# Gate and up products by seven block products in place of eight, in a two-layer hybrid decoder trunk

## The chip, the cores and the metric

The kernel runs on one core of a Trainium2 chip. The metric is the device time of one execution in microseconds (us). The engines go by the profile's names: PE is TensorE (PEld its weight loads), DVE is VectorE, ACT is ScalarE, POOL is GpSimd, SP is the engine that issues the transfers.

## What is computed

Two layers, each of a mixer (latent attention beside a state space part) and a feed-forward part, over 512 rows of 1024 columns in float32. The change concerns the feed-forward part:

```
h = rmsnorm(x, norm2_w[l]) * (1.0 + sc2) + sh2
x = x + g2 * swiglu(h, w_gate_up[l], w_down[l])

def swiglu(h, w_gate_up, w_down):
    g, u = jnp.split(h @ w_gate_up, 2, axis=-1)
    return (jax.nn.silu(g) * u) @ w_down
```

The inner width is 2816, which is 22 tiles of 128. The six modulation vectors of a layer (sh2, sc2, g2 among them) come from a product of the condition c with a 1024 x 6144 matrix.

## The kernel before, in words

Activations lie transposed: the 1024 columns on 8 tiles of partitions, the 512 rows along the free dimension (xT, hh, hl). Every float32 product is made of three matmuls of a reduced format: each operand is split into hi (a cast, on ACT) and lo (source minus hi, on DVE or POOL), and `mm3` (L317) adds hi·hi, hi·lo and lo·hi in PSUM. A weight tile of 128 columns is 512 KB; `wload` (L304) has SP load it into one of three raw buffers, ACT cast it to hi and DVE or POOL subtract to lo; a table of bits says which of the two.

The second norm's sums of squares and the hidden are made half by half (`HALVES`, 256 rows each). `out_proj` gives the second half of the mixer's output; beside it the first half's hidden is made. Then `nst`, a matmul with ones, gives the second half's mean square, ACT and DVE turn it into a row scale, and `hid` (L420) makes the hidden per k: one step on DVE (ht), one cast with a bias on ACT (hh), one step on DVE (hl).

`ffn` (L1013) then runs over f, the 22 tiles of the inner width. Per f there is a gate tile and an up tile, each 8 blocks of k, three matmuls of 512 columns per block: 48 matmuls. ACT takes silu of the gate's PSUM (sg), DVE multiplies by the up's PSUM, and `split` (L440) makes ah and al, of which all 22 tiles are kept. The first two tiles are run in halves (`mtiles_halves`, L449), so that the first half's matmuls can run while the second half's hidden is made. From f = 2 on, layer 0 also loads the next layer's modulation matrix, three tiles per f, 48 in all; each costs DVE a multiply with a sum (`ada1`, rawa). At last the down products run: 8 tiles m of 22 blocks of k, 66 matmuls of 512 columns each (dps), the last m in halves, and DVE adds each to xT.

The order on each engine is the scheduler's, which places instructions by their data; only the mixer's part is pinned. PSUM has five banks of the kind mm and three of the kind ms here.

## Time and profile before

| | |
|---|---|
| time, median of 3 executions | 1289.55 us (1289.34 to 1289.65) |
| span of the profiled execution | 1284.9 us |
| mean granted PE clock, core 0 | 0.974 |
| PE busy | 1211.4 us (94%) |
| DVE, ACT, POOL busy | 634.1, 519.9, 531.1 us |
| gate and up products, layer 0 | from 306.25 to 550.29 us |
| gate and up products, layer 1 | from about 916 to 1158.29 us |
| down products, layer 1 | from 1158.29 to the end |

The span is the time from the first to the last instruction of one profiled execution. The times of a row are starts from the beginning of the span, with a duration; a matmul's duration is longer than its distance from the next one, because matmuls are pipelined, so costs of PE are read as distances from start to start. "granted clock" is 1.00 where PE runs at 2.4 GHz and falls towards 0.5 where it runs at 1.2 GHz.

### The profile page before, as it was taken

To read this page: it belongs to the slowest core of one execution; us is meant where nothing else is said; L and a number is where in the kernel's file an instruction comes from. 1 tells how busy PE (TensorE), PEld (TensorE's weight loads), DVE (VectorE), ACT (ScalarE), POOL (GpSimd) and SP (SyncE) were. 2 spreads that over 40 slices of the span, in tenths; PEclk is the share of its full clock that TensorE was granted. 3 is DMA by queue.
4 is the path that set the end of the run, shared out by engine and by line. 5 is a ranking of instruction groups with operands and counts; after the bars stand their busy time and mean duration, and the time that the engine had idled before them with its cause. 6 is when DMAs were issued, how large, how long until landed. Compare 5 with 4: busy or idle time off the path is not lost. (4 is left out here: it accounts for less than half of the span.)

```text
span 1284.9 us, 16463 instructions
## 1 busy us (share of the span) xinstructions
PE 1211.4 (94%) x6343; PEld 1005.1 (78%) x6344; DVE 634.1 (49%) x1128; ACT 519.9 (40%) x896; POOL 531.1 (41%) x310
## 2 busy tenths in 40 slices
PE   6889796889999999999998999979999999999998
PEld 6768674689888888888887887659988888888888
DVE  6979778879245545211128885576821111110100
ACT  4366774435322222222226668654532222222110
POOL 2651145263676666523333232346333333333231
PEclk9899898899999999999999899999999999999999
DMA  9433352464477777423223222103333332323331
GB/s 321 154 125 102 114 164 99 150 200 143 129 241 238 239 240 237 134 87 97 96 71 107 83 79 70 34 33 91 124 115 99 90 106 84 102 94 107 115 101 40
DMA packets 47855, 162.34 MB, mean 126 GB/s; under 512 B 5344, under 2 KB 8224, under 8 KB 47776
## 3 DMA queue, kind: packets, MB, share of 16 engines
q1 hardware_dynamic: 47776, 161.29, 38.8%
q8 instruction: 50, 0.82, 0.3%
q14 instruction: 29, 0.24, 0.1%
HBM read 159.14 MB, written 2.13 MB: 126 GB/s over the span
## 5 line engine op out<-in xcount | busy, mean ns | idle before, releaser
L292 POOL TENSOR_TENSOR lo<-raw,hi 128x1024 fp32r<-128x1024 f32 x108 | 272.6, 2524 | 338.6 <-ACT hi L156 338.5
L156 ACT CAST hi<-raw 128x1024 fp32r<-128x1024 f32 x179 | 188.0, 1051 | 500.8 <-issue 183.5
L140 PE MATMUL gup<-hl,hi 128*128 128x512 f32 (+1 forms) x736 | 280.4, 381 | 0.0
L140 PE MATMUL gup<-hh,lo 128*128 128x512 f32 (+1 forms) x736 | 279.9, 381 | 0.0
L140 PE MATMUL gup<-hh,hi 128*128 128x512 f32 (+1 forms) x736 | 278.6, 381 | 0.0
L156 DVE TENSOR_TENSOR lo<-raw,hi 128x1024 fp32r<-128x1024 f32 x71 | 88.9, 1253 | 152.6 <-ACT hi L156 150.8
L140 PEld LDWEIGHTS gup<-hh,lo 128*128 128x128 f32 x736 | 139.1, 189 | 26.5
L140 PEld LDWEIGHTS gup<-hl,hi 128*128 128x128 f32 x736 | 139.0, 189 | 26.0 <-DVE hl L156 0.2
L140 PEld LDWEIGHTS gup<-hh,hi 128*128 128x128 f32 x736 | 138.4, 189 | 26.2
L156 DVE SCALAR_TENSOR_TENSOR rawa<-rawa,cb 128x1024 f32<-128x1024 f32 x77 | 111.0, 1443 | 76.7 <-DMA rawa<-wada 76.5
L140 PE MATMUL dps<-ah,hi 128*128 128x512 f32 x308 | 121.8, 396 | 0.0
L140 PE MATMUL dps<-al,hi 128*128 128x512 f32 x308 | 121.8, 396 | 0.0
L140 PE MATMUL dps<-ah,lo 128*128 128x512 f32 x308 | 121.8, 396 | 0.0
L156 DVE TENSOR_TENSOR sg<-sg,gup 128x512 f32<-128x512 f32 x44 | 30.3, 688 | 179.6 <-PE gup L140 173.5
L440 POOL TENSOR_TENSOR al<-sg,ah 128x512 fp32r<-128x512 f32 x44 | 67.6, 1535 | 97.2 <-ACT ah L156 93.6
L140 PE MATMUL ops<-hh,hi 128*128 128x256 f32 x256 | 74.4, 290 | 3.1 <-ACT hi L156 1.5
L140 PE MATMUL ops<-hl,hi 128*128 128x256 f32 x256 | 72.5, 283 | 1.0 <-POOL hl L440 1.0
L140 PE MATMUL wps<-hh,hi 128*128 128x512 f32 x168 | 70.8, 422 | 2.4 <-DVE xbc L156 2.4
L140 PE MATMUL ops<-hh,lo 128*128 128x256 f32 x256 | 72.5, 283 | 0.3 <-POOL lo L292 0.3
L140 PEld LDWEIGHTS dps<-al,hi 128*128 128x128 f32 x308 | 57.9, 188 | 14.1
L140 PEld LDWEIGHTS dps<-ah,hi 128*128 128x128 f32 x308 | 57.9, 188 | 14.0
L140 PEld LDWEIGHTS dps<-ah,lo 128*128 128x128 f32 x308 | 57.9, 188 | 13.9
(303 smaller groups left out, 2103.3 us busy)
## 6 DMA issues: line engine op xcount, KB each, us to landing
raw<-ws SPq DMA_DIRECT2D x181, 512.0 KB, 3.5
rawa<-wada SPq DMA_DIRECT2D x80, 512.0 KB, 4.4
raws<-wada SPq DMA_DIRECT2D x16, 512.0 KB, 5.3
ar<-ard SPq DMA_DIRECT2D x8, 512.0 KB, 3.9
rawk<-ws SPq DMA_DIRECT2D x8, 404.0 KB, 5.4
xT<-xin SPq DMA_DIRECT2D x8, 256.0 KB, 5.9
out<-xT SPq DMA_DIRECT2D x7, 256.0 KB, 2.6
rawr<-ws SPq DMA_DIRECT2D x4, 424.0 KB, 3.2
```

What stands on the lines that cost most here:

```text
L140: self._put(self.tc.nc.tensor.matmul(out, lhsT, rhs, **kw), 4 * n if rhs.dtype == F32 else n)
L156: i = f(*args, **kw)
L292: (eng or ve).tensor_tensor(lo[:, :n], raw[:, :n], hi[:, :n].bitcast(F32), op=ALU.subtract)
L440: (eng or ve).tensor_tensor(lo, src, hi.bitcast(F32), op=ALU.subtract)
```

## The change

The gate and up matrices together are a 2 x 2 block matrix: two halves of the inputs' 1024 columns by the gate and the up tile of one f. The hidden is a 2 x 2 block matrix too: two halves of the columns (k 0 to 3, 4 to 7) by two halves of the rows (H0, H1). Strassen's scheme, in Winograd's form, makes the four result blocks from seven products of blocks rather than eight. Per f there are now seven products of 4 blocks of k and three matmuls of 256 columns, 84 matmuls. In their place come sums of blocks: of the hidden once per layer (B12−B11, B22−B11, B22−B12 and one more, `ts`), of the weights per f (`sums_a`, `sums_b`, four sums of 512 columns on DVE), each then split into hi and lo, and of the results per f (`c11`, `c12`, `c22`, `first`, on 256 columns, after copies on ACT). The PSUM tiles are gx (products 1, 6, 7, 4 one after another, read in between), gy (product 2) and gz (products 5, 3); p5 is a copy of gz after product 5. Before product 3 may add into gz, that copy must have been made.

The gate tile's own hi and lo (hiu, lou) come from three different ways: lo on DVE for f = 0, on POOL for f = 1 and 2, and from f = 3 on as a negated copy of the raw tile on ACT and a transfer issued by POOL that reads the same weights from memory and adds them (`accum_op`). The lower half of the up tile is split by ACT and POOL (vh, vl).

The 22 tiles of ah and al are no longer kept: `PIECES` cuts them into 6, 6, 5 and 5, and after each piece its rows of W_down are multiplied, 8 tiles m of 6 or 5 blocks of k, and added to xT. W_down is laid out in 32 tiles of up to 6 blocks in place of 22 of 8. Only the last piece's last three m run in halves. The next layer's modulation tiles are loaded at other places: in each iteration of the first piece, at odd f after that, and in the down products; eight of them are left for layer 1. PE, DVE and ACT are held in the written order from behind nst to the last piece's last three m (`te.pinned = ve.kept = se.kept = True`). PSUM has banks mm 4, my 2, ms 2. The diff's core:

```diff
+PIECES = ((0, 6), (6, 12), (12, 17), (17, 22))
-    def ffn(l, h):
+    def ffn(l, mix, nrm2, kept):
...
-            for f in range(FT):
-                sg = T(f"sg{l}{f}")
-                gps = gu(2 * f)
-                i = se.activation(sg, gps, AF.Silu)
-                if f > 1:
-                    ada_some(1, fp, i)
-                ups = gu(2 * f + 1)
-                i = ve.tensor_tensor(sg, sg, ups, op=ALU.mult)
-                split(ah[:, f, :], al[:, f, :], sg, ge)
-                if f > 1:
-                    ada_some(2, fp, i)
...
+            def weights(b, name, eng, n=8, t=None):
+                if t is None:
+                    t = load(b, name, n)
+                hi, lo = (wp.tile([P, 8, P], F32R, name=f"{x}{name}", tag=x) for x in ("hi", "lo"))
+                se.copy(hi[:, :n], t[:, :n])
+                if eng is None:
+                    se.activation(lo[:, :n], t[:, :n], AF.Identity, scale=-1.0)
+                    ge.dma_start(lo[:, :n], ws[l, b].rearrange("p (k m) -> p k m", m=P)[:, :n], accum_op=ALU.add)
+                else:
+                    eng.tensor_tensor(lo[:, :n], t[:, :n], hi[:, :n].bitcast(F32), op=ALU.subtract)
+                return hi, lo
...
+            def sums_a(f):
+                if f < FT:
+                    g, u = raw[f]
+                    t, hi = pair(f, 5, 6)
+                    ve.tensor_tensor(t[:, 0:K4], u[:, 0:K4], u[:, K4:KT], op=ALU.add)
+                    ve.tensor_tensor(t[:, K4:KT], t[:, 0:K4], g[:, 0:K4], op=ALU.subtract)
+                    se.copy(hi, t)
...
+            def rest(f, i, eng=None):
+                if f < FT:
+                    t, hi, lo = sf[f, i]
+                    (eng or ve).tensor_tensor(lo, t, hi.bitcast(F32), op=ALU.subtract)
...
+            def product(i, f):
...
+                for k in range(K4):
+                    mm3(ps, whi[:, k], wlo[:, k], xhi[:, k], xlo[:, k], k == 0 and i in (1, 2, 5), k == K4 - 1,
+                        skip_group_check=True)
+                if i == 5:
+                    p5[f] = fp.tile([P, HW], F32, name=f"p5{l}_{f}", tag="p5", bufs=2)
+                    se.copy(p5[f], ps)
...
+            te.pinned = ve.kept = se.kept = True
+            for i in (1, 2):
+                product(i, 0)
+            for k in range(K4):
+                nrm2.apply((None, None), rb2, H1, (k,), full=full(k, 1), pool=hpool)
+            c11(0)
+            ve.tensor_tensor(b[11], b[12], b[11], op=ALU.subtract)
+            se.copy(hh[:, 0:K4, H1], b[11])
+            for i in (1, 2):
+                product(i, 1)
+            loads(2)
+            gate_weights(2, ge)
+            for k in range(K4, KT):
+                nrm2.apply(hid_hl, rb2, H1, (k,), full=full(k, 1), pool=hpool)
+                if k == K4:
+                    ve.tensor_tensor(hl[:, 0:K4, H1], b[11], hh[:, 0:K4, H1].bitcast(F32), op=ALU.subtract)
+            c11(1)
+            ve.tensor_tensor(b[11], b[22], b[11], op=ALU.subtract)
+            split(*ts[2], b[11])
+            sums_b(1)
+            for i in (1, 2):
+                product(i, 2)
+            c11(2)
+            rest(1, 3)
+            ve.tensor_tensor(b[12], b[22], b[12], op=ALU.subtract)
+            split(*ts[3], b[12], ge)
+            up_weights(1)
+            for i, f in ((5, 0), (5, 1), (3, 0), (3, 1), (6, 0)):
+                product(i, f)
...
+                    for f in range(max(c0, 3), c1):
+                        if f > c0 + 1:
+                            product(4, f - 2)
+                            first(f - 2, c0, ah, al)
+                        if f > c0:
+                            up_weights(f)
+                        if f < c1 - 1:
+                            loads(f + 2)
+                        product(1, f)
+                        sums_a(f + 1)
+                        product(2, f)
+                        c11(f)
+                        rest(f + 1, 5)
+                        product(5, f)
+                        if f > c0:
+                            product(7, f - 1)
+                            c22(f - 1)
+                        if f < c1 - 2:
+                            gate_weights(f + 2)
+                        else:
+                            fetch(f - c1 + 2)
+                        sums_b(f + 1)
+                        product(6, f)
+                        product(3, f)
+                        c12(f)
+                        rest(f + 1, 3)
+                        silu(f)
+                        if c0 == 0 or f % 2:
+                            ada_some(1)
```

Below, rows of the instruction order of the two kernels; a row is the line, the operation, the tile written and the tiles read, and the size. The first place is ACT at the start of layer 0's feed-forward part. Before, from the last of the first half's hidden (ht_0) over the row scale (na) to the second half's hidden (ht_256):

```order
L156 ACTIVATE hh<-ht_0_2920,mods_92 128x256
L156 ACTIVATE na_256_2926<-nst_256_2924,eps 128x256
L156 ACTIVATE na_256_2926<-na_256_2926 128x256
L156 ACTIVATE hh<-ht_256_2932,mods_92 128x256
L156 ACTIVATE hh<-ht_256_2936,mods_92 128x256
```

And of the kernel after, the last 12 of the 22 rows that stand between the row scale and the copy p5 of f = 0 (p_0); b are the blocks of the hidden, t2h and t3h the hi of two block sums, sh_1_3 that of a weight sum, vh_1 that of an up tile:

```order
L154 ACTIVATE hh<-ht_256_3091,mods_92 128x256
L154 ACTIVATE b_2643<-ht_256_3096,mods_92 128x256
L154 ACTIVATE hh<-ht_256_3096,mods_92 128x256
L154 ACTIVATE b_2643<-ht_256_3101,mods_92 128x256
L154 ACTIVATE hh<-ht_256_3101,mods_92 128x256
L154 COPY sg_3106<-gy_1_3064 128x256
L154 CAST t2h_2631<-b_2640 128x1024
L154 CAST sh_1_3_3113<-sf_1_3_3112 128x1024
L154 COPY sg_3144<-gy_2_3131 128x256
L154 CAST t3h_2633<-b_2641 128x1024
L154 CAST vh_1_3151<-rawxv_1_2987 128x512
L154 COPY p_0_3168<-gz_0_3155 128x256
```

Between the row scale and the first copy out of gz there now stand casts of block sums, of weights and of an up tile, each of them behind the one above it.

The second place is DVE in the middle of layer 1's gate and up products. Before, it has the multiply by the up tile's PSUM and a weight tile's lo now and then:

```order
L156 TENSOR_TENSOR sg_8344<-sg_8344,gup_8383 128x512
L156 TENSOR_TENSOR lo_39_8482<-raw_39_8479,hi_39_8481 128x1024
L156 TENSOR_TENSOR sg_8411<-sg_8411,gup_8450 128x512
L156 TENSOR_TENSOR lo_42_8581<-raw_42_8578,hi_42_8580 128x1024
L156 TENSOR_TENSOR sg_8478<-sg_8478,gup_8517 128x512
```

After, the iteration f = 8 of layer 1 on DVE, from the weight sums of tile 9 to the last step of tile 7:

```order
L154 TENSOR_TENSOR sf_9_5_10733<-rawv_9_10591 128x512
L154 TENSOR_TENSOR sf_9_5_10733<-sf_9_5_10733,rawg_9_10589 128x512
L154 TENSOR_TENSOR sg_10752<-sg_10752,gx_8_10720 128x256
L154 TENSOR_TENSOR sl_9_5_10735<-sf_9_5_10733,sh_9_5_10734 128x1024
L154 TENSOR_TENSOR p_7_10642<-p_7_10642,gx_7_10593 128x256
L154 TENSOR_TENSOR sg_10625<-sg_10625,p_7_10642 128x256
L154 TENSOR_TENSOR sf_9_3_10790<-rawg_9_10589,sf_9_5_10733 128x512
L154 TENSOR_TENSOR sf_9_3_10790<-rawg_9_10589,rawv_9_10591 128x512
L154 TENSOR_TENSOR sg_10752<-sg_10752,gx_8_10720 128x256
L154 TENSOR_TENSOR sl_9_3_10792<-sf_9_3_10790,sh_9_3_10791 128x1024
L154 TENSOR_TENSOR sg_10625<-sg_10625,gx_7_10593 128x256
```

Eleven steps per f stand where one or two stood, and two of them (sl) read what ACT casts (sh) from sums that stand above them. ACT's rows beside it, from silu of tile 7 to silu of tile 8, in the third place:

```order
L154 ACTIVATE sg_10625<-sg_10625 128x512
L154 CAST ah_9688<-sg_10527 128x512
L154 CAST vh_8_10712<-rawxv_8_10493 128x512
L154 CAST sh_9_5_10734<-sf_9_5_10733 128x1024
L154 COPY sg_10752<-gy_8_10739 128x256
L154 COPY p_8_10769<-gz_8_10756 128x256
L154 CAST hiu_10_10785<-rawg_10_10716 128x1024
L154 ACTIVATE lou_10_10786<-rawg_10_10716 128x1024
L154 CAST sh_9_3_10791<-sf_9_3_10790 128x1024
L154 COPY sg_10752<-gz_8_10756 128x256
L154 ACTIVATE sg_10752<-sg_10752 128x512
```

Before, ACT had four rows per f there, in a repeating row of a silu, two casts of weights (hi) and a cast of the activations (ah):

```order
L156 ACTIVATE sg_8344<-gup_8351 128x512
L156 CAST hi_39_8481<-raw_39_8479 128x1024
L156 CAST ah_8026<-sg_8344 128x512
L156 CAST hi_40_8513<-raw_40_8511 128x1024
L156 ACTIVATE sg_8411<-gup_8418 128x512
```

It now has ten, among them two copies out of PSUM (gy, gz) on which DVE's sums into sg wait.

## Rows read from the trace of the kernel before

**Rows 1.** The page, busy time, share of the span and instructions by engine.
```profile
PE 1211.4 (94%) x6343; PEld 1005.1 (78%) x6344; DVE 634.1 (49%) x1128; ACT 519.9 (40%) x896; POOL 531.1 (41%) x310
```

**Rows 2.** Chain that ended last: start, us, engine, tile, line, count; layer 1.
```profile
916.97 2.38 DVE acc L156
...
920.09 238.20 PE gup L140 x1088
1158.29 107.80 PE dps L140 x462
1266.09 7.80 PE dps17mm L140 x66
```

**Rows 3.** Windows: stretch, us, busy PE, PEld, DVE, ACT, POOL, clock, DMA, GB/s.
```profile
310.10:318.00 7.90, 7.84 (x50) 7.75 (x51) 7.26 (x19) 3.94 (x9) 0.00 (x0) 0.78 0.24 66
320.00:550.00 230.00, 230.00 (x1026) 190.88 (x1026) 99.65 (x130) 69.33 (x87) 143.80 (x62) 1.00 0.62 206
...
932.00:1158.20 226.20, 226.20 (x1000) 187.30 (x999) 40.73 (x43) 67.04 (x87) 82.23 (x42) 1.00 0.32 99
```

**Rows 4.** Timeline, PE, layer 0's gate and up: start, us, engine, line, operation, idle before.
```profile
400.01 0.39 PE L140 MATMUL gup<-hh,hi 128*128 128x512 f32 x1
400.24 0.39 PE L140 MATMUL gup<-hl,hi 128*128 128x512 f32 x1
```

**Rows 5.** Timeline, PE, layer 0's output projection, 256 columns, first and eleventh of a row.
```profile
303.01 0.28 PE L140 MATMUL ops<-hh,hi 128*128 128x256 f32 x1
...
304.21 0.28 PE L140 MATMUL ops<-hl,hi 128*128 128x256 f32 x1
```

**Rows 6.** Timeline, start of layer 0's feed-forward part, PE, then DVE, then ACT.
```profile
310.16 0.70 PE L140 MATMUL nst<-acc,ones 128*128 128x256 f32 x2 [1.82 <-DVE acc L156]
...
311.40 0.42 PE L140 MATMUL gup<-hh,hi 128*128 128x256 f32 x1
311.62 0.41 PE L140 MATMUL gup<-hl,hi 128*128 128x256 f32 x1
...
313.29 1.26 DVE L156 SCALAR_TENSOR_TENSOR ht<-xT,gn,nst 128x256 f32<-128x256 f32 x3
...
313.81 1.31 ACT L156 ACTIVATE hh<-ht,mods 128x256 fp32r<-128x256 f32 x3 [1.93 <-DVE ht L156]
```

**Rows 7.** Groups by line and form from 320 us on: count, busy, mean ns, idle before.
```profile
L156 DVE TENSOR_TENSOR lo<-raw,hi 128x1024 fp32r<-128x1024 f32 x50 | 62.8, 1257 | 115.3 <-ACT hi L156 113.5
L156 DVE TENSOR_TENSOR sg<-sg,gup 128x512 f32<-128x512 f32 x43 | 29.6, 688 | 170.8 <-PE gup L140 164.7 <-ACT sg L156 6.1
L156 DVE SCALAR_TENSOR_TENSOR ht<-xT,gn,nst 128x256 f32<-128x256 f32 x32 | 14.1, 474 | 0.2
...
L156 ACT CAST hi<-raw 128x1024 fp32r<-128x1024 f32 x154 | 161.9, 1052 | 486.7 <-issue 183.5 <-PE gup L140 161.6 <-PE dps L140 127.4
L156 ACT CAST ah<-sg 128x512 fp32r<-128x512 f32 x44 | 27.4, 623 | 0.0
...
L156 ACT ACTIVATE hh<-ht,mods 128x256 fp32r<-128x256 f32 x32 | 14.9, 500 | 13.0 <-DVE ht L156 13.0
```

**Rows 8.** Timeline, DVE and POOL in layer 0's gate and up products.
```profile
398.87 1.22 DVE L156 SCALAR_TENSOR_TENSOR rawa<-rawa,cb 128x1024 f32<-128x1024 f32 x1
399.12 3.23 POOL L292 TENSOR_TENSOR lo<-raw,hi 128x1024 fp32r<-128x1024 f32 x1 [3.05 <-ACT hi L156]
...
402.31 1.29 POOL L440 TENSOR_TENSOR al<-sg,ah 128x512 fp32r<-128x512 f32 x1
404.56 2.39 POOL L292 TENSOR_TENSOR lo<-raw,hi 128x1024 fp32r<-128x1024 f32 x1 [0.96 <-ACT hi L156]
404.72 2.25 DVE L156 TENSOR_TENSOR mods<-mods,sm 128x8 f32<-128x8 f32 x1
```

**Rows 9.** The page, queues (packets, MB, share of 16 engines) and issues (KB, us to landing).
```profile
q1 hardware_dynamic: 47776, 161.29, 38.8%
...
raw<-ws SPq DMA_DIRECT2D x181, 512.0 KB, 3.5
```

More of the change, by code (lines that the diff above doesn't have):

```diff
@@ L67 @@
     'OA': (0x82, 0xda),
-    'FW': (0xf, 0x6),
-    'FD': (0xc, 0xe),
     'WU': 18,
@@ L73 @@
     'STK': 2,
-    'FO': (1, 0),
 }
@@ L94 @@
 B_IN, B_UP, B_OUT, B_GU, B_DN = 0, 16, 19, 27, 71
-NBLK = 93
+PIECES = ((0, 6), (6, 12), (12, 17), (17, 22))
+NBLK = 71 + 8 * len(PIECES)
 NR = 424
@@ L334, in ada1 @@
         nc.sync.dma_start(r2, wada[l, t])
-        if te.pinned and t > 15 and PLAN['AD'] & 1 << t - 16:
+        if te.pinned and not ve.kept and t > 15 and PLAN['AD'] & 1 << t - 16:
             n_ = PLAN['AGH']
@@ L415, in hidden, with apply, hid @@
             self.apply(h, self.scale(sl), sl)
-        def apply(self, h, rb, sl, ks=range(KT)):
+        def apply(self, h, rb, sl, ks=range(KT), **kw):
             for k in ks:
-                hid(self.l, self.which, h, k, rb, sl)
-    def hid(l, which, h, k, rb, sl=slice(0, S), eng=None):
+                hid(self.l, self.which, h, k, rb, sl, **kw)
+    def hid(l, which, h, k, rb, sl=slice(0, S), eng=None, full=None, pool=tp):
         o = 0 if which == 1 else 8
@@ L425, in hid @@
         hh, hl = h
-        t = T(f"ht{l}{which}{k}_{sl.start}")
         n = sl.stop - sl.start
+        t = T(f"ht{l}{which}{k}_{sl.start}", [P, n] if pool is not tp else None, pool=pool, **({"bufs": 4} if pool is not tp else {}))
         ve.scalar_tensor_tensor(t[:, :n], xT[:, k, sl], gn[l][:, o + k:o + k + 1], rb[:, :n], op0=ALU.mult, op1=ALU.mult)
+        if full is not None:
+            se.activation(full, t[:, :n], AF.Identity, bias=sh)
+        if hh is None:
+            return
         se.activation(hh[:, k, sl], t[:, :n], AF.Identity, bias=sh)
@@ L447, in mtile @@
         return ps
-    def mtiles_halves(l, bs, h, names):
-        ws_ = [wload(l, b) for b in bs]
-        pss = [bank("mm", n) for i, n in enumerate(names)]
-        for sl in HALVES:
-            for k in range(KT):
-                for (hi, lo), ps in zip(ws_, pss):
-                    mm3(ps[:, sl], hi[:, k, :], lo[:, k, :], h[0][:, k, sl], h[1][:, k, sl], k == 0, k == KT - 1)
-        return pss
     def mixer(l, h, rows, first):
@@ L1186, in trunk @@
             ada_some(1)
-        with psum(f"f{l}", **(dict(ms=3, mm=5) if PLAN['FO'][l] else dict(mm=5, ms=3))):
-            h = hid_hl
-            rb = None
-            for i, _ in enumerate(out_proj(l, mix, nrm, HALVES[1], kept)):
-                if i % KT == KT - 1:
-                    i //= KT
-                    if i == 0:
-                        rb = nrm.scale(HALVES[0])
-                    else:
-                        nrm.apply(h, rb, HALVES[0], (i - 1, i) if i == KT - 1 else (i - 1,))
-            nrm.hidden(h, HALVES[1])
-            if l == 0:
-                ada_q.extend([(1, t) for t in range(48)])
-            h = ffn(l, h)
+        with psum(f"f{l}", mm=4, my=2, ms=2):
+            h = ffn(l, mix, nrm, kept)
 def _pack(inp):
@@ L1270, in _pack @@
         dn = mt(a["w_down"][l])
-        dn = dn.transpose(0, 2, 1, 3).reshape(22, 8, P, P).transpose(0, 2, 1, 3)
-        ws[l, B_DN:B_DN + 22] = dn
+        for i, (a0, a1) in enumerate(PIECES):
+            ws[l, B_DN + 8 * i:B_DN + 8 * i + 8, :, :a1 - a0] = dn[:, :, a0:a1]
         wada[l] = a["w_ada"][l].T.reshape(48, P, D)
```

254 lines of the change are left out of this document (204 added, 50 removed).

## The prediction

> **What bounds the kernel now.** I read the totals by engine first: PE is busy 1211.4 us of a span of 1284.9 us, DVE 634.1, ACT 519.9, POOL 531.1 [rows 1]. Then the chain that ended last: in layer 1 it is one unbroken piece of PE from the gate and up products to the end of the down products, 238.20 and 107.80 us long, behind a short DVE step [rows 2]. The windows say the same of both layers: PE works 230.00 of 230.00 us (layer 0) and 226.20 of 226.20 us (layer 1) at a granted clock of 1.00, while DVE has 99.65 and 40.73 us of work, ACT 69.33 and 67.04, POOL 143.80 and 82.23 [rows 3]. So in the feed-forward part PE is the only limit, nothing else is near it, and PE work that goes away is worth its full length there, as long as the others keep up with what replaces it.
>
> **PE's gain.** A 512-column step takes 0.2267 us start to start [rows 4], so one tile pair takes 48 × 0.2267 = 10.88 us. A 256-column step takes 0.120 us in the stretch of the output projection (ten steps in 1.20 us) [rows 5]; the 256-column steps of the last down tile are 7.80/66 = 0.118 apart [rows 2]. I take 0.1195. Seven products of 12 steps are 84 × 0.1195 = 10.04 us. A layer goes from 96 × 0.12 + 1008 × 0.2267 = 240.0 to 22 × 10.04 = 220.8 us: 19.2 us less, **38.4 us in two layers**. Strassen saves an eighth of the columns, but two half-width steps cost 0.239 where one full step costs 0.2267, so 7.7% is left. The bounds: 0.118 per step would give 5 us more, 0.120 2 us less. The down products keep their number (528 steps per layer, 0.2333 each by 107.80/462 [rows 2]); I cost their new order at nothing.
>
> The trace's two steps differ by 5.5% per column. The Trainium skill's page "TensorE: Matmul & The Clock Gate" (Part 1, "Wait — 56ns, not 53.3ns?") gives a start-to-start distance at the full clock of the columns over 2.4 GHz and about 2.5 ns more, that is 109 and 216 ns; by it the gain would be 1.19 rather than 0.84 us per tile pair and the sum 15 us lower, some 1320 us. The trace shows 120 and 227 ns at a granted clock of 1.00, so the sum goes by the trace; I give the rule 1 in 20, inside the forecast's own chance.
>
> **The price at the start.** Before, the second half's hidden needs only, per k, one DVE step, one cast on ACT and one DVE step: nst at 310.16, the row scale ready by 313.29, the first three ht steps take 1.26 us, ACT's casts run beside them [rows 6]. PE stood 1.82 us before nst, and then ran part of the time at half the clock (steps of 0.21 us for 256 columns) [rows 6], since 310.1 to 318 has a mean granted clock of 0.78 [rows 3]. All that the start lost is some 3 us.
>
> After, the half must first become block sums: B12−B11, B22−B11, B22−B12, each split into hi and lo, and DVE and ACT are held in the written order. PE has only the six products 1 and 2 (f = 0, 1, 2) and two products 5 before product 3 of f = 0, 8 × 1.43 = 11.5 us. That product waits for the copy p5 (p_0 in the order), the last of 22 ACT rows. I walk the two engines from the moment the row scale is there (R), with 256-wide steps of DVE at 0.39 apart and of ACT at 0.41 to 0.50, 1024-wide ones at 1.22 to 1.26 (DVE) and 1.05 (ACT) [rows 6 to 8], and 0.05 per hand-over:
>
> - four ht on DVE and four b on ACT behind them, GY copy: R+2.6; sum with gx and B12−B11 on DVE: R+4.2; cast on ACT: R+5.3; cast of gate tile 2: R+6.25.
> - now four rounds ht → b, hh → hl, each about 1.7 us, since each hl stands before the next ht on DVE, and one 1024-wide subtract in between: R+13.7. Then GY copy, sum, B22−B11: R+15.2; cast t2h R+16.3; t2l and two 512-wide sums R+18.7; cast R+19.8; GY copy, sum, lo, B22−B12: R+22.9; cast t3h, cast vh, p5: **R+25**.
> - GpSimd's lo of gate tile 2 starts at R+6.3 and DVE's hl beside it has two operands in SBUF. Such pairs exclude one another in the trace: POOL's lo took 3.23 rather than 2.39 us behind a DVE step that ended at 400.09, and a 128x8 step of DVE took 2.25 us beside POOL's lo [rows 8]. This adds up to 1.6: R+25 to R+26.6.
>
> R comes 3.1 us behind nst as before, up to 6.7 if the other sums on DVE stand in front. So product 3 starts about nst+30 and PE has 11.5 us of work: **17 to 18 us idle**, of which 5 to 6 before product 1 of f = 2 (waiting for its lo from GpSimd). Behind it PE needs 17 products (24.4 us) up to product 3 of f = 3, but waits for the sum c12 of f = 1 behind two ACT casts (2.3 us), and 6 us for gate tile 3: its hi and negated copy are written behind the silu of f = 2 on ACT, and then an accumulating DMA must land. No such DMA is in the trace; the nearest row is a plain load of the same 512 KB, 3.5 us [rows 9], and I take 4, with ACT's two steps ahead of it 6. The Trainium skill's page "DMA: Bandwidth & Descriptors" (Anatomy of one DMA — SWDGE (gpsimd) path) has 2.0 us and bytes over 436 GB/s, so 3.2 us as an estimate; no run here shows it, and the sum would be under 2 us lower. With about 2 us of half clock the start costs 17.5 + 8.5 + 2 = 28 us, **25 more than before in each layer, 50 in all**. Bounds per layer: if DVE were never late, its own work to B22−B12 is 15 us, and with R at 3.1 and the last three ACT rows PE would stand 9 us, with 10 for the rest: 16 net; with the late R and full exclusion, 33.
>
> **The price in the loop.** From f = 3 on, DVE has per tile five 256-wide steps, four 512-wide and two 1024-wide: 5 × 0.47 + 4 × 0.69 + 2 × 1.26 = 7.6 us, 6.8 with the overlap of neighbours that the three ht steps show (1.26 us rather than 3 × 0.47) [rows 6, 7]; ACT has 4 × 1.05 (two sums' hi, the gate's hi and its negated copy), 3 × 0.62 (silu, ah, vh) and three copies of 0.45, 7.4 us; POOL 1.3 [rows 8] and the DMA's issue. None is over PE's 10.04. But twice in an iteration DVE stands behind ACT for a cast and a copy that themselves wait for DVE's sums (sf → sh → copy → sg, then sl): 2 × 1.5 us. That closes a ring of 9.8 us, and 10.5 when POOL's vl (512 columns, 1.29 us like al [rows 8]) locks one 1024-wide step out. Where a modulation load comes in (a 1024-wide DVE step, 1.22 us [rows 8], and its landing), the iteration takes 11.8 to 13.2: three times in the first piece of each layer, and at odd f in layer 0. PE has a slack of some 4 us that fills within a piece; what is behind by then shows at the end of the piece, where product 7 of the last f waits for c12 with one product (1.43 us) as cover. I reckon 2.5 us and 1 us for the end in each of layer 1's four pieces, and 3 more in its first, 17 or, less what the down products' cover gives back, **11**; in layer 0 some 5 us per piece, **19**. Together **30 us**, bounds 6 and 48.
>
> **Small things.** The loads of the down tiles in pieces (32 of up to 384 KB rather than 22 of 512 KB) fit under 4.2 us of PE per tile; with modulation loads in the same buffers up to 4 us. Edges between the layers 0 to 4. I take **4**.
>
> **The sum.** The profiled execution spans 1284.9 us; 4.65 us lie outside against the median 1289.55. 1284.9 − 38.4 + 50 + 30 + 4 = 1330.5, and with 4.65 **1335 us**.
>
> **Rivals.**
> - *PE keeps its gain* (faster): the start's ring runs at DVE's pace and the second part finds its data, so that PE stands 9 us at the start, 6 more than before, and the loop's ring of 9.8 us stays under PE's 10.04: 1289.55 − 38.4 + 12 + 5 = 1268 us. For it: no engine has 10 us of work per iteration, and the sums are at bounds that rows allow. Against it: the written order on DVE and ACT and the hl/ht rounds. It decides at 19.2 us per layer of new waits; below that the change pays. Chance 0.14.
> - *Even*: both at their lower bounds, −38.4 + 32 + 6 + 0: 1289 us. Chance 0.04.
> - *The accumulating DMA sets the pace*: a gate tile's lo is issued some 13 us before its product; if issue and landing take longer than that under the load of the other transfers, every iteration from f = 3 waits. At 2 us per iteration for 2 × 19 iterations on top of 1335 it is 1411 us. For it: a kind of transfer that the trace doesn't have. Against: plain landings of 3.5 us, a queue with a busy share of 38.8% [rows 9]. Chance 0.07.
> - *The forecast*: waits at the start and in the loop exceed the gain. Chance 0.75, own range 1297 to 1372.
>
> **Chances and range.** Faster 0.14, within 0.2% (which is about what a measurement of this kernel can tell from no change) 0.04, slower 0.82. From the lower bounds (1289) to the upper ones, −38.4 + 66 + 48 + 10 = 1375: I take 1290 to 1373, which leaves most of the first rival and of the third out.
>
> **What would show it.** In the changed profile: 256-column steps of 0.118 to 0.120 us (the gain); two idle stretches of PE within 30 us of nst, 5 to 6 us ended by GpSimd's lo and about 12 us ended by ACT's p5; then 6 us ended by the DMA's lo of f = 3; iterations of layer 1 within 10.0 to 10.6 us and those with a modulation load 1 to 3 us longer; waits of product 7 for DVE's sg at the ends of pieces. If the start costs less than 19 us more than before per layer and layer 1's iterations are at 10.0, the forecast is wrong and the first rival holds.

## The result, and the profile after

The kernel after takes 1452.78 us (median; 1451.43 to 1455.87) against 1289.44 us of the kernel before beside it: a ratio of 1.1295, 95% interval 1.1257 to 1.1332. It is slower by 163 us, where 46 were forecast and 1373 us was the range's upper end. The direction was right, the size was not.

The page of the kernel after, busy time by engine, as in [rows 1]; the span is now 1449.7 us:

```profile
PE 1225.0 (84%) x7790; PEld 1086.1 (75%) x7790; DVE 959.4 (66%) x1639; ACT 685.2 (47%) x1210; POOL 428.1 (30%) x319
```

PE's busy sum is hardly changed: behind its idle stretches PE's steps run in part at half the clock (1.2 GHz; the mean granted clock of the start is 0.76, below) and take longer. Steps at full clock cost what they did in [rows 5]; timeline of PE in layer 1, two steps at the ends of a row of twelve distances:

```profile
1389.74 0.28 PE L138 MATMUL gx<-t3l,sh 128*128 128x256 f32 x1
...
1391.18 0.28 PE L138 MATMUL gx<-t2l,sh 128*128 128x256 f32 x1
```

That is 1.44/12 = 0.120 us a step. So the gain came as forecast. What PE waited for, from the view of waits (engine, tile, releaser: us in total, times, longest):

```profile
PE gx L138 <- DVE sg L154: 62.1, 28, 6.0
PE gz L138 <- ACT p L154: 20.3, 2, 10.4
PE nst L138 <- DVE acc L154: 18.9, 5, 5.9
PE gx L138 <- ACT hiu L154: 13.8, 4, 6.0
PE gx L138 <- DMA lou<-ws: 12.3, 2, 6.2
PE rps L138 <- DVE ht L154: 11.6, 1, 11.6
```

The stretches, as windows, beside [rows 3] (stretch, length, busy of PE, PEld, DVE, ACT, POOL, granted clock, DMA share, GB/s). Layer 0: the start, the first piece's down products, pieces 2 and 3 (gate and up) with the down products between them; then layer 1: start, and pieces 2 and 4:

```profile
315.20:380.00 64.80, 37.76 (x242) 36.15 (x241) 38.94 (x55) 31.67 (x51) 19.04 (x11) 0.76 0.23 65
...
416.50:453.00 36.50, 35.49 (x160) 28.63 (x160) 25.00 (x35) 8.76 (x11) 4.02 (x3) 1.00 0.74 231
453.00:531.60 78.60, 66.59 (x493) 65.58 (x492) 46.77 (x70) 37.18 (x57) 18.46 (x15) 0.89 0.55 142
531.60:566.60 35.00, 35.00 (x158) 28.54 (x157) 24.62 (x39) 8.68 (x11) 4.11 (x3) 1.00 0.78 253
566.60:630.00 63.40, 52.82 (x409) 51.98 (x408) 39.67 (x60) 30.46 (x48) 14.73 (x12) 0.92 0.57 151
```

```profile
1033.00:1096.00 63.00, 35.33 (x236) 33.73 (x235) 38.11 (x55) 30.24 (x49) 17.68 (x10) 0.77 0.23 67
...
1182.70:1248.20 65.50, 60.83 (x494) 60.22 (x493) 42.99 (x64) 37.26 (x58) 18.59 (x15) 0.97 0.56 141
...
1367.20:1416.80 49.60, 48.89 (x410) 48.64 (x410) 30.66 (x47) 29.30 (x46) 14.46 (x12) 1.00 0.55 138
```

In layer 1's last piece five tiles take 49.6 us and PE is busy nearly all of it: 9.9 us per tile in place of 10.88 before. There the change does what it was forecast to do. The same work takes 63.4 us in the third piece of layer 0, with no engine near its limit.

The whole difference by stretches. PE's own work is counted as 1.434 us per product (12 × 0.1195) and 0.2333 us per down step; the rest of a stretch is loss. The ends are the first product, product 1 of f = 3 with its lo, and the last down step.

| stretch (us) | layer 0 | layer 1 | forecast, layer 0 and 1 |
|---|---|---|---|
| later begin of layer 0's feed-forward part (306.25 to 315.19) | 8.9 | | 0 |
| start: length; loss | 62.7; 35.2 | 62.2; 34.7 | loss 28; 28 |
| rest of the pieces: length; loss | 381.8; 65 | 351.3; 34 | loss 19; 11 |
| last down step to layer 1's first product, against before | | 273.1 − 241.5 = 31.6 | 4 with all edges |
| PE's gain, both layers | | −38.4 | −38.4 |
| what the kernel before lost in these stretches | | −7.3 | −6 |

The sum is 164 us, and the spans differ by 164.8. Of the 65 us that the pieces of layer 0 lose, 42 are waits of PE; the other 23 are mostly PE's steps at half the clock behind these waits. In layer 1 it is 24 and 10.

### The profile page after: what moved, and what is told of

Its sections match the earlier page's. It is cut to its first block, busy times and chain, and to the rows that moved or that the text cites. A ratio compares the mean times of both kernels' runs of the same rounds, so it can differ in the third digit from the quotient of the medians.

```text
span 1449.7 us, 20376 instructions
## 1 busy us (share of the span) xinstructions
PE 1225.0 (84%) x7790; PEld 1086.1 (75%) x7790; DVE 959.4 (66%) x1639; ACT 685.2 (47%) x1210; POOL 428.1 (30%) x319
## 5 line engine op out<-in xcount | busy, mean ns | idle before, releaser
L154 ACT CAST sh<-sf 128x1024 fp32r<-128x1024 f32 x88 | 91.9, 1044 | 107.2 <-DVE sf L154 96.9
L138 PE MATMUL dps<-ah,lod 128*128 128x512 f32 x322 | 127.5, 396 | 1.0 <-DMA lod<-ws 1.0
L138 PE MATMUL dps<-ah,hid 128*128 128x512 f32 x322 | 127.7, 397 | 0.0
L138 PE MATMUL dps<-al,hid 128*128 128x512 f32 x322 | 127.4, 396 | 0.0
L138 PE MATMUL gz<-hh,sh 128*128 128x256 f32 x352 | 105.0, 298 | 20.3 <-ACT p L154 20.3
L154 DVE TENSOR_TENSOR sl<-sf,sh 128x1024 fp32r<-128x1024 f32 x84 | 114.6, 1364 | 7.4 <-ACT sh L154 7.4
L138 PE MATMUL gz<-hh,sl 128*128 128x256 f32 x352 | 104.0, 296 | 0.9 <-DVE sl L154 0.9
L138 PE MATMUL gz<-hl,sh 128*128 128x256 f32 x352 | 103.7, 295 | 0.0
L138 PEld LDWEIGHTS gz<-hh,sh 128*128 128x128 f32 x352 | 73.2, 208 | 20.7 <-ACT p L154 20.7
L138 PEld LDWEIGHTS gz<-hh,sl 128*128 128x128 f32 x352 | 71.8, 204 | 1.3 <-DVE sl L154 1.3
```

What stands on the lines that cost most here:

```text
L138: self._put(self.tc.nc.tensor.matmul(out, lhsT, rhs, **kw), 4 * n if rhs.dtype == F32 else n)
L154: i = f(*args, **kw)
```

## Experiments

Times are medians; the ratios to the kernel before, measured beside each, are what is compared (1.1295 for the kernel after). Stretches are read from one profile of each run, and a stretch in which a run changes nothing differs by some us: from layer 0's last down step to layer 1's first product it is 273.1 us in the kernel after and 271.3, 267.6 and 269.2 in e3_start, e8_start_rows and e12_warm.

### The modulation tiles

The iterations of layer 0 with a modulation tile are long and those without are not. Timeline of PE, the first steps of product 1 of f = 8 to 11 in layer 0 (modulation tiles are multiplied at the ends of f = 7 and 9):

```profile
476.11 0.28 PE L138 MATMUL gx<-hh,hiu 128*128 128x256 f32 x1
...
491.07 0.28 PE L138 MATMUL gx<-hh,hiu 128*128 128x256 f32 x1
...
501.06 0.28 PE L138 MATMUL gx<-hh,hiu 128*128 128x256 f32 x1
...
515.84 0.28 PE L138 MATMUL gx<-hh,hiu 128*128 128x256 f32 x1
```

15.0 us for f = 8, 10.0 for f = 9 and 14.8 for f = 10, against 10.0 each in layer 1. Timeline from the end of f = 9 into f = 10, DVE, the queue of SP, then PE:

```profile
498.37 0.68 DVE L154 TENSOR_TENSOR sf<-rawg,rawxv 128x512 f32<-128x512 f32 x1
499.08 0.33 SPq L332 DMA_DIRECT2D rawa<-wada  x1
...
500.83 1.22 DVE L154 TENSOR_TENSOR sl<-sf,sh 128x1024 fp32r<-128x1024 f32 x1
...
505.19 1.23 DVE L154 SCALAR_TENSOR_TENSOR rawa<-rawa,cb 128x1024 f32<-128x1024 f32 x1 [3.14 <-DMA rawa<-wada]
...
509.94 0.39 PE L138 MATMUL gx<-t2h,sh 128*128 128x256 f32 x1 [3.02 <-DVE sg L154]
```

The load is issued when the last sum over raw weights (ended 499.05) frees a buffer. DVE comes to its multiply at 502.05 and stands for 3.14 us, and the sums for the next tile stand behind it. PE is then idle before product 6, which adds into gx and must wait until DVE has read gx (`c11`). The wait is 3.0 of the 4.8 us that f = 10 is too long. The rest is PE's steps behind it, which run at half the clock. Windows, the iteration and the 3 us behind the wait, columns as above:

```profile
501.06:515.84 14.78, 11.76 (x87) 11.56 (x86) 7.86 (x12) 3.25 (x6) 2.88 (x2) 0.88 0.54 157
509.94:513.00 3.06, 3.06 (x16) 3.06 (x17) 3.02 (x5) 0.00 (x0) 0.50 (x1) 0.58 0.48 151
```

In the kernel before, DVE stood for these loads too, but PE was busy throughout [rows 3]. Timeline of DVE before, in layer 0's gate and up products:

```profile
396.37 1.23 DVE L156 SCALAR_TENSOR_TENSOR rawa<-rawa,cb 128x1024 f32<-128x1024 f32 x1 [2.56 <-DMA rawa<-wada]
```

**e1_no_mod**, 1394.12 us, ratio 1.0832 (1.0794 to 1.0870):

```
-        if l == 1:
-            ada_q.extend([(1, t) for t in range(40, 48)])
+        ve.memset(mods[l][:, 40:48], 0.5)
+        ada_fin(l, 40, 48)
+        ada_q.clear()
...
-                            ada_q.extend([(1, t) for t in range(40)])
+                            ve.memset(mods[1][:, 0:40], 0.5)
...
```

> Leaves out every modulation tile that the feed-forward parts load and multiply (8 of layer 0's own and 48 of layer 1's; constants stand in their place), the rest is the changed kernel. Theory: a modulation tile's load starts when a raw buffer comes free and DVE waits for it in the written order, so its iterations are 5 us too long; without it layer 0's pieces come down to what layer 1's later pieces lose (about 5 us each): 48 us less in layer 0, 13 less in layer 1's first piece, some 10 less at the edges, 1380 us (1365 to 1395). Rival, the ring between DVE and ACT as forecast: only DVE's own 1.25 us per tile go, some 15 to 25 us, 1430 us or more.

The time fell by 59 us, to the slow end of the theory's range; the rival is out. By the table's count layer 0's pieces lose 24.5 in place of 65 us, layer 1's 23 in place of 34, the edge 20.6 in place of 31.6. The starts lose what they did, 35.3 and 34.8.

**e6_mod_dve**, 1401.98 us, ratio 1.0907 (1.0871 to 1.0942), and **e7_mod_load**, 1398.03 us, ratio 1.0873 (1.0835 to 1.0910), split the loop's part in two. Both also leave out what e1_no_mod leaves out, the tiles in the down products among it:

```
-                        if c0 == 0 or f % 2:
-                            ada_some(1)
+                        if c0 == 0 or (l == 0 and f % 2):
+                            ve.tensor_reduce(tiny(f"mw{l}_{f}", 1), cb, axis=AX.X, op=ALU.add)
```

and in e7 a load into `wraw(...)` in place of the sum.

> As the run without modulation (the same tiles left out), but where the loop would multiply a modulation tile DVE sums up 1024 columns of data that lie on chip: DVE's work of some 1.2 us without a load. Theory: DVE's work alone is taken up by PE's slack: 1398 us (1392 to 1408), within 10 us of the run without modulation. Rival, the ring between DVE and ACT is full and each 1.2 us shows with what follows: 1415 us or more.

> As the run without modulation, but where the loop would multiply a modulation tile it is only loaded, into one of the raw buffers, and not read: the buffer and the transfer without DVE's work. Theory: the wait comes from both together, a load that starts late and an engine that must wait for it in order; the load alone delays the next weight tile by less than its slack: 1400 us (1392 to 1412). Rival, the raw buffers are the limit and the weight tiles come late: 1420 us or more.

DVE's work alone cost about 8 us and the load alone about 4 (its interval overlaps that of e1). Together with the tiles in the down products they cost 59. The closest comparison is that of the four iterations of layer 0 in the middle of a piece that follow a tile at odd f (f = 8, 10, 14 and 20). They take 40.0 us in e1, 3.6 more with the work alone, 0.3 more with the load alone and 21.2 more in the kernel after. So neither the work nor the transfer alone is the price there. What is left is an engine that waits in a fixed order for a load that starts late; e10_own_buffer below tests that.

**e5_mod_down**, 1452.1 us, ratio 1.1293 (1.1248 to 1.1339):

```
-                        if c0 == 0 or f % 2:
+                        if c0 == 0:
...
-                        ada_some(2 if m == 3 and c1 < FT else 1)
+                        ada_some(2 if m % 2 and c1 < FT else 1)
```

> All modulation tiles are loaded and multiplied, but those at odd f of layer 0's last three pieces are moved to the down products (twelve per piece rather than nine). Theory: the loss is DVE waiting for a late load in the written order while PE needs DVE's sums at once; under the down products PE needs DVE little, so most of the 39 us that layer 0's last three pieces lose to modulation go: 1422 us (1412 to 1435). Rival, the amount of loads and multiplies counts wherever it stands: 1445 us or more.

The theory failed here, and the time is the rival's. The iterations that held the moved tiles fell to 10.0 us each, but the first one after each piece rose to 18 to 21. Timeline of this kernel, DVE, SP's queue and PE behind the first down products:

```profile
460.10 1.23 DVE L154 SCALAR_TENSOR_TENSOR rawa<-rawa,cb 128x1024 f32<-128x1024 f32 x1 [2.66 <-DMA rawa<-wada]
...
461.36 0.33 SPq L332 DMA_DIRECT2D rawa<-wada  x1
464.93 1.23 DVE L154 SCALAR_TENSOR_TENSOR rawa<-rawa,cb 128x1024 f32<-128x1024 f32 x1 [3.60 <-DMA rawa<-wada]
...
470.01 0.58 PE L138 MATMUL gx<-t2h,sh 128*128 128x256 f32 x1 [11.16 <-DVE sg L154]
```

DVE goes from one late load to the next and falls behind PE by up to 11 us. The waits moved with the tiles, and they cost the same at the next point where PE needs DVE. The rival's reason, the amount of loads and multiplies, does not follow: e10_own_buffer has the amount of e9_pieces5 and takes 22 us less.

**e9_pieces5**, 1467.56 us, ratio 1.1411 (1.1381 to 1.1441), is the control for **e10_own_buffer**, 1445.33 us, ratio 1.1241 (1.1216 to 1.1266):

```
-PIECES = ((0, 6), (6, 12), (12, 17), (17, 22))
+PIECES = ((0, 5), (5, 10), (10, 14), (14, 18), (18, 22))
...
-                        ada_some(2)
+                        ada_some(3)
```

and in e10 also

```
+                        if (c0 == 0 or f % 2) and ada_q:
+                            ad = fp.tile([P, 8, P], F32, name=f"rawa{l}_{f}", tag="rawa", bufs=1)
+                            nc.sync.dma_start(ad.rearrange("p a b -> p (a b)"), wada[ada_q[0][0], ada_q[0][1]])
...
-                        if c0 == 0 or f % 2:
-                            ada_some(1)
+                        if ad is not None:
...
```

> The changed kernel with five pieces of 5, 5, 4, 4 and 4 tiles in place of four of 6, 6, 5 and 5; it is the control for the next one, since it leaves 4 KB free on each partition. Theory: a piece's end costs some 6 us whatever its length, so one more in each layer: 1463 us (1456 to 1475). Rival, the loss goes by iterations with a modulation tile alone: no change, 1450 to 1455 us.

> As the run with five pieces, but the modulation tiles of the loop (not those of the down products) have a buffer of their own, and their load is written at the start of the iteration. Theory: what costs 5 us in these iterations is that the load waits for a raw buffer, holds it until DVE comes to it, and DVE stands in the written order before it; with an own buffer layer 0's odd iterations fall from 15 to under 11 us: 30 to 40 us less than with five pieces, some 1428 us (1418 to 1440). Rival, transfers as such are too slow there, or DVE's work is too much: within 12 us of the run with five pieces.

The fifth piece costs some 15 us. With a buffer of its own the tile at odd f no longer makes an iteration longer than 10.9 us (14.8 to 16.6 with five pieces alone). That shows the cause for the loop's tiles, though not how much of it is the buffer and how much the earlier issue. 22 us are gone, less than the theory's 30. The tiles in the down products still load through the raw buffers, and the first iterations of the second to fourth piece stay at 14 to 17 us (16 to 18 with five pieces alone).

### The start

**e8_start_rows**, 1440.07 us, ratio 1.1202 (1.1161 to 1.1243):

```
-                nrm2.apply(hid_hl, rb2, H1, (k,), full=full(k, 1), pool=hpool)
...
+                ve.scalar_tensor_tensor(t, xT[:, k, H1], gn[l][:, 8 + k:9 + k], rb2[:, :HW], op0=ALU.mult, op1=ALU.mult)
+                se.activation(full(k, 1), t, AF.Identity, bias=sh)
+                se.activation(hh[:, k, H1], t, AF.Identity, bias=sh)
...
+            for k in range(K4, KT):
+                ve.scalar_tensor_tensor(hl[:, k, H1], hts[k], mods[l][:, 24 + k:25 + k], hh[:, k, H1].bitcast(F32),
+                                        op0=ALU.add, op1=ALU.subtract)
```

> The changed kernel, with the second half's hidden at the start made in rows: four ht on DVE, the casts behind them, then four hl, in place of four rounds of ht, cast, hl. Theory: the start is the sum of hand-overs on one path, the rounds take 6.8 us of it and the rows some 3.5: 3.3 us less per layer and some half clock, 1444 us (1440 to 1448). Rival, the start hangs on something else (the lo of gate tile 2 on POOL, the loads): no change, 1451 to 1455 us.

The start took 59.3 and 57.0 us in place of 62.7 and 62.2, and the wait before product 3 fell from 9.98 to 4.84 us in layer 0. The theory holds in kind. The time fell by 12.7 us where it said 8.8, and 8.6 of them lie in the two starts, in place of 6.6.

**e3_start**, 1451.16 us, ratio 1.1277 (1.1246 to 1.1308):

```
+            ve.tensor_tensor(hl[:, 0:K4, H1], b[11], hh[:, 0:K4, H1].bitcast(F32), op=ALU.subtract)
             loads(2)
             gate_weights(2, ge)
...
+                if k == K4 + 1:
+                    product(5, 0)
+            product(3, 0)
+            for i in (1, 2):
+                product(i, 2)
...
+            product(5, 1)
+            product(6, 0)
...
```

> Another written order at the start: products 5 and 3 of f = 0 stand ahead of products 1 and 2 of f = 2, and the copy p5 of f = 0 ahead of half of the hidden; product 6 of f = 0 ahead of the second weight sum. Theory: the start's length is the sum of DVE's and ACT's steps, so the 10 us wait before product 3 goes but a part comes back before product 6 or 7: 4 to 9 us less per layer, 1437 us (1430 to 1446). Rival, the place of p5 alone makes the wait: all of 10 us per layer goes and the half clock behind it, 1425 us or less.

Both missed: no change that the time shows. The start is 62.7 us in both layers, against 62.7 and 62.2. The 10 us wait is gone; in layer 0 4.64 and 1.39 us now stand before products 5 and 3 of f = 0 and 5.82 us before product 7 of f = 1. So the length is that of the path through DVE and ACT, wherever PE's products stand in it.

**e12_warm**, 1443.48 us, ratio 1.1221 (1.1192 to 1.1251):

```
...
+            warm(44)
             for i in (1, 2):
                 product(i, 2)
...
+                if (i, f) == (3, 0):
+                    warm(80)
```

> The changed kernel, with 44 and 80 matmuls of 256 columns without use written into the two long waits of PE at the start of each layer's feed-forward part (5 and 10 us). Theory: some 8 us of the start's 35 us are PE's steps at half the clock behind these waits; kept busy, PE goes on at full clock and the start is 3 to 6 us shorter per layer: 1444 us (1438 to 1449). Rival, PE's steps there lie beside the longer path of DVE and ACT, and the clock costs nothing: no change, or some us more where the filling overruns, 1451 to 1458 us.

The time fell by 9 us, into the theory's range, yet not for its reason: from the first product to the last down step layer 0 took 441.3 us in place of 444.5 and layer 1 412.9 in place of 413.4; the rest lies in the mixer and the edge, where nothing was changed. The mean granted clock of the start rose from 0.77 in both layers to 0.92 and 0.89, and the start got 2.1 and 0.6 us shorter. Only some 3 us can be put down to the clock there: PE's slow steps lie beside the path of DVE and ACT.

**e2_pool_lo**, 1473.89 us, ratio 1.1437 (1.1395 to 1.1479):

```
-                gate_weights(3)
+                gate_weights(3, ge)
...
-                gate_weights(4)
+                gate_weights(4, ge)
...
-                            gate_weights(f + 2)
+                            gate_weights(f + 2, ge)
```

> The lo of the gate tiles from f = 3 on by a subtract on POOL in place of ACT's negated copy and the accumulating DMA (but for the reloaded tiles at the pieces' ends). Theory: only the wait at f = 3, 6 us per layer, hangs on that DMA; POOL's 2.4 us of subtract lock a step of DVE out now and then: 1445 us (1435 to 1455). Rival, the accumulating DMAs set the loop's pace: 20 us less or more, under 1433.

Neither held: it is slower by some 18 us. The start got 3 us shorter, but layer 1's iterations rose from 10.0 to 11.3 and 11.9 us. Timeline of this kernel, DVE and then POOL in layer 1:

```profile
1310.99 1.78 DVE L154 TENSOR_TENSOR sf<-rawv 128x512 f32<-128x512 f32 x1
...
1316.81 2.17 DVE L154 TENSOR_TENSOR sg<-sg,p 128x256 f32<-128x256 f32 x1
```

```profile
1310.79 1.44 POOL L1091 TENSOR_TENSOR vl<-rawxv,vh 128x512 fp32r<-128x512 f32 x1 [0.80 <-ACT vh L154]
1316.15 2.54 POOL L1046 TENSOR_TENSOR lou<-rawg,hiu 128x1024 fp32r<-128x1024 f32 x1 [3.92 <-ACT hiu L154]
```

A 256-wide step of DVE took 2.17 us in place of 0.42 beside POOL's lo, as in [rows 8]. The Trainium skill's page "SBUF — State Buffer" (SBUF: two separate sides) has it that a DVE step with two SBUF operands and a POOL step that reads SBUF share a pair of ports, which whichever starts first holds for its whole length; these rows agree. I read the longer iterations as the ring of the forecast, 9.8 us and what POOL adds, and the accumulating DMA as what keeps POOL's subtract out of it and the ring under PE's 10.04. The run shows the longer iterations and the long DVE steps; the ring itself is argued.

### The pieces and the edge

**e4_pieces_only**, 1302.54 us, ratio 1.0116 (1.0091 to 1.0141):

```
-                    cur[n // 8] = wload(l, B_DN + n // 8, eng=ge if PLAN['FD'][l] & 1 << n // 8 % 4 else None)
+                    cur[m] = wload(l, B_DN + KT * pc + m, n=c1 - c0, eng=ge if PLAN['FD'][l] & 1 << m % 4 else None)
...
+            for pc, (c0, c1) in enumerate(PIECES):
+                for f in range(c0, c1):
...
+                for m in range(KT if c1 < FT else KT - 1):
+                    ps = bank("mm", f"dps{l}{pc}_{m}")
```

> The kernel before with the activations in four pieces, each multiplied by its rows of W_down at once (the change's tiles of W_down, its adds to xT), and nothing of the seven products; the modulation stays where it was. Theory: cutting into pieces costs PE nothing within a layer and some us at the edge to layer 1, where the sums of squares now come within the last piece: 1295 us (1290 to 1306). Rival, the pieces are a large part of the loss: 1330 us or more.

The time is in the theory's range, but higher than its 1295 and in part for another reason: it is 15 us, of which 5.5 are a wait of the next layer's first products, as it said, and 7.6 waits of down products for al at the pieces' ends, where it had nothing. The rival is out: by themselves the pieces are a small part.

**e13_banks**, 1444.72 us, ratio 1.1237 (1.1196 to 1.1277). In the kernel after, timeline of PE at the edge (idle time and its releaser at the end):

```profile
766.18 1.22 PE L138 MATMUL nst<-acc,ones 128*128 128x256 f32 x2 [4.73 <-DVE acc L154]
767.58 0.72 PE L138 MATMUL rps<-hir,hh 128*128 128x424 f32 x1 [0.18 <-ACT hh L154]
...
780.87 0.72 PE L138 MATMUL rps<-hir,hh 128*128 128x424 f32 x1 [11.58 <-DVE ht L154]
```

One chunk's steps of the first k run, and the next waits for the last ht of the other half, which it doesn't read.

```
-        with psum(f"f{l}", mm=4, my=2, ms=2):
+        with psum(f"f{l}", **(dict(ms=2, mm=4, my=2) if l == 0 else dict(mm=4, my=2, ms=2))):
```

> The changed kernel, with the banks of PSUM in another order in layer 0's feed-forward part (ms first, as the kernel before has it there), so that the next layer's first products don't fall on the bank that holds the second half's row scale. Theory: PE's wait of 11.6 us behind the first rps steps goes, 9 to 14 us less with the half clock behind it: 1441 us (1437 to 1446). Rival, the hidden itself is late and PE waits for it in any bank: no change, 1450 to 1456 us.

In this kernel's timeline the same steps follow one another:

```profile
774.35 1.07 PE L138 MATMUL rps<-hir,hh 128*128 128x424 f32 x2 [0.18 <-ACT hh L154]
775.22 0.56 PE L138 MATMUL rps<-hir,hl 128*128 128x424 f32 x1
775.58 0.56 PE L138 MATMUL rps<-lor,hh 128*128 128x424 f32 x1
```

The wait is gone, and the stretch from the last down step to layer 1's first product is 254.0 us in place of 273.1 (267.6 to 273.1 in runs that leave it as it was). The order of the banks was the cause of the wait. The time fell by 8 us only, and the intervals overlap: layer 0's feed-forward part came out 4 us longer, layer 1's 4 us longer, and layer 0's began 2 us later in this run, which is not explained.

**e11_norm_dve**, 1456.53 us, ratio 1.1334 (1.1300 to 1.1368):

```
-                                    nrm.add(m, s2)
+                                    nrm.add(m, s2, ve)
```

> The changed kernel, with the next layer's sums of squares added up on DVE in place of POOL in the last piece. Theory: the edge between the layers is long because POOL's adds, POOL's weight splits and DVE's steps stand behind one another at the last piece's end: 4 to 8 us less, 1446 us (1442 to 1450). Rival, the last tiles come late by themselves (modulation loads in the down products): no change, 1451 to 1455 us.

No change that can be told from the kernel after: the wait of rps for ht is 12.5 us in it, as the bank makes it. POOL's adds were not the cause.

**e14_three**, 1376.06 us, ratio 1.0698 (1.0651 to 1.0744), joins the edits of e1_no_mod, e8_start_rows and e13_banks.

> Three edits together: no modulation in the feed-forward parts (as the run without modulation, its tiles left out), the hidden at the start in rows, the banks in the other order. Theory: the causes lie in different stretches and add up: 1394 less 12 less 12, 1371 us (1364 to 1380). Rival, they hide one another: 1382 us or more.

They add up to 77 us, against 59, 13 and 8 each by itself, within the theory's range. What is left of the loss: the starts 31.9 and 31.5 us, the pieces 27 and 22, the edge 11.6, the later begin 10.3. No version with the seven products came near the kernel before, even without the modulation.

## Why the prediction was wrong

**PE's gain** was right: 38.4 forecast, and the later pieces of layer 1 run at 10.0 us per tile.

**The start** was right in its steps and short by 7 us per layer. PE's waits were forecast at 17 to 18 us before product 3 of f = 0 and 8.5 behind it; measured in layer 0 (timeline of PE, idle before the step):

```profile
328.72 0.58 PE L138 MATMUL gx<-hh,hiu 128*128 128x256 f32 x1 [5.63 <-ACT hiu L154]
331.14 0.58 PE L138 MATMUL gx<-hh,lou 128*128 128x256 f32 x1 [1.62 <-POOL lou L1046]
349.11 0.58 PE L138 MATMUL gz<-hh,sh 128*128 128x256 f32 x1 [9.98 <-ACT p L154]
360.47 0.39 PE L138 MATMUL gx<-t3h,sh 128*128 128x256 f32 x1 [2.03 <-DVE sg L154]
377.86 0.58 PE L138 MATMUL gx<-hh,lou 128*128 128x256 f32 x1 [6.24 <-DMA lou<-ws]
```

17.2 before product 3, and 9.8 behind it: 2.0, 6.2, 1.1 before product 1 of f = 3 (for hiu) and 0.5 in between. So the waits came out nearly as forecast. The path was longer because the row scale came later than I took it, 8.1 us behind nst's begin at 1032.14 in layer 1 rather than 3.1 to 6.7: POOL splits two weight sums there, and DVE's steps to the row scale stand still. Timeline of DVE and POOL:

```profile
1035.74 1.88 DVE L154 SCALAR_TENSOR_TENSOR na<-na 128x256 f32<-128x256 f32 x1
1037.66 2.52 DVE L154 SCALAR_TENSOR_TENSOR nst<-na 128x256 f32<-128x256 f32 x1
1040.21 1.66 DVE L154 SCALAR_TENSOR_TENSOR ht<-xT,gn,nst 128x256 f32<-128x256 f32 x4
```

```profile
1034.51 5.38 POOL L1084 TENSOR_TENSOR sl<-sf,sh 128x1024 fp32r<-128x1024 f32 x2 [4.48 <-ACT sh L154]
```

PE filled the longer path with steps at half the clock, 8 us (35.2 of loss less 27.1 idle), where I had counted 2 as a cost of their own; by e12_warm, which kept the clock up and shortened the start by 2.1 and 0.6 us, they hardly are one. The accumulating DMA took 5.8 us from issue to landing in the page of the kernel after, where I took 4 from a plain load's 3.5 in [rows 9].

**The loop** is the step that failed: 30 us forecast, 99 measured. I had the ring of DVE and ACT as its price. If there is one, it lies under PE's time (10.0 us per iteration without a modulation tile); only e2_pool_lo, with more work on POOL, has longer ones. The price was in two other terms. The first is the modulation tile, which I had at 1 to 3 us: in layer 0 a tile's iteration is 5 us longer, some 3 of wait and 1.8 of steps at half the clock, for which the loop's sum had nothing. Without modulation (e1_no_mod) some 51 of the 99 us are gone. I read the load's landing as part of the iteration and did not follow the raw buffers: three and one, where the kernel before has two more for modulation alone. A load can start only when a weight tile's buffer is read out, and DVE waits for it where the order puts it. The second term is the end of a piece. In e1_no_mod layer 1's pieces still lose 23 us, some 6 each, where I had 2.5 and 1 and took part of that back; both layers lose 48 without any modulation tile, against 30 for all. There, too, an engine stands for a load, here ACT for that of a down tile (rawd, of which hid is the hi). Timeline of ACT in e1_no_mod, layer 1:

```profile
1164.16 0.38 ACT L154 COPY p<-gz 128x256 f32<-128x256 f32 x1
1171.35 0.83 ACT L154 CAST hid<-rawd 128x768 fp32r<-128x768 f32 x1 [6.82 <-DMA rawd<-ws]
```

The first down tile's load was issued at 1168.43, when the last sum over raw weights had ended (1168.39), and ACT stands before its cast, with the cast of the weight sum (sh) behind it; DVE then waits 5.77 us, and PE 0.98 before product 7 and 2.91 before the next product 6. This is read from the trace; no run gives these loads an earlier issue or a buffer of their own. I also put PE's slack at product 7, some 4 us, and missed that product 6 of the same f waits for c11: two products (2.87 us) of cover.

**The edges** were forecast at 4 us and measured at 40, 8.9 of them ahead of layer 0's first product. Two causes I did not look for. Ahead of nst DVE now has the first tiles' sums and splits, and the last sum of squares stands behind them; two of these steps are long beside POOL's. In both layers nst waits 5.94 us rather than 1.82 as in [rows 6]. Timeline of layer 0, DVE, POOL, then PE:

```profile
307.72 2.59 DVE L154 SCALAR_TENSOR_TENSOR hl<-ht,mods,hh 128x256 fp32r<-128x256 f32 x1
307.67 2.36 POOL L1046 TENSOR_TENSOR lou<-rawg,hiu 128x1024 fp32r<-128x1024 f32 x1 [0.96 <-ACT hiu L154]
314.54 1.22 PE L138 MATMUL nst<-acc,ones 128*128 128x256 f32 x2 [5.94 <-DVE acc L154]
```

No run takes these steps out from ahead of nst, so this cause is argued. And the banks of PSUM are in another order, so that the next layer's first products fall on the one that holds the row scale. The diff shows that order in one line. The wait for it took 11.6 us, as e13_banks shows. The rest of the 40 is not taken apart.

**The rivals.** Of the first rival's sign half came: layer 1's iterations without a modulation tile are at 10.0 us, but the start cost 32 us more than before per layer, not under 19. The accumulating DMA does not set the pace: its wait shows at f = 3 only. The measured time lies above every time that the prediction names, 1411 us the highest. My upper bound for the loop, 48 us, was the sum of my own terms at their worst; it held no case in which a resource that I had not followed ran out.

## What to carry to other kernels

Where engines are held in a written order, the price of a load can be not its transfer but the wait of the engine that comes to it too early, and of all that stands behind it there; follow each buffer from its last reader to the next load before costing a loop. Here moving such a wait to another place (e5_mod_down) or PE's work around it (e3_start) changed nothing; an own buffer with an earlier issue (e10_own_buffer) and a shorter path (e8_start_rows) did. A wait of PE can also cost more than its length, when the steps behind it run at half the clock. And a stretch that nobody meant to change can pay: an order of banks decides whose last reader the next stage waits for.

## What the runs showed of the hardware

A DMA that adds into SBUF, issued by POOL, took 5.8 us (median of 26) from issue to landing for 512 KB, against 3.5 to 3.6 for plain loads of gate and up tiles of that size in the same execution (4.3 for those of the modulation tiles). The estimate from the Trainium skill's page "DMA: Bandwidth & Descriptors" (Anatomy of one DMA — SWDGE (gpsimd) path) in the prediction was 3.2 us; the measurement decides, and it is longer.

```profile
rawg<-ws SPq DMA_DIRECT2D x44, 512.0 KB, 3.6
lou<-ws POOLq DMA_DIRECT2D x26, 512.0 KB, 5.8
```

Filling PE's waits with steps of no use (e12_warm) raised the granted clock of the start from 0.77 to 0.92 and 0.89 and shortened it by 2.1 and 0.6 us only. In the start DVE and ACT set the length, as e3_start shows. In the loop it looks otherwise: behind a wait of 3.0 us the granted clock was 0.58, and f = 10 of layer 0 came out 1.8 us longer than the wait accounts for. No run keeps the clock up there.
